# The next layer's modulation inside the first merge: condition rows in PSUM, loads two steps ahead, products to a buffer of their own, another count of steps per slot

## Chip, cores, metric

One core of one Trainium2 chip runs the whole program. The metric is the device time of one execution, in microseconds (us).

## What is computed

A backbone of two layers (DEPTH = 2) over 1024 latent tokens and 256 context tokens, width 1024, float32. Each layer normalises and modulates its input, projects it once, runs four token mixers r = 0..3 (pooling, latent attention, differential attention, windowed attention), gates and merges them and projects out:

```python
shift, scale, gate = jnp.split(jax.nn.silu(c) @ w_mod + b_mod, 3, axis=-1)
shift_c, scale_c, gate_c = jnp.split(jax.nn.silu(c_ctx) @ w_mod + b_mod, 3, axis=-1)
h = rms_norm(x, g_pre) * (1 + scale[:, None, :]) + shift[:, None, :]
z = split_cols(h @ w_in)
...
m = sum(mgate[:, :, r] * ((ys[r] * gates[:, :, r]) @ w_br[r]) for r in range(N_BRANCH))
x_new = x + gate[:, None, :] * rms_norm(m @ w_out, g_post)
```

mgate is the sigmoid of 4 x 1024 columns of z, gates the silu of 4 x 256 others. Two condition vectors, c and c_ctx, multiply the same w_mod: silu(c) and silu(c_ctx) are "the two condition rows". The gate of layer 0 (1024 columns) and shift, scale and gate of layer 1 (3072 columns) are needed only after the merge of layer 0, and it is these that the changed code computes.

## The kernel before

**The merge of layer 0** is one loop over 32 pairs (r, d), counted here as q = 0..31: branch r = q // 8, block d = q % 8 of 128 output columns. In each q TensorE makes three chunks of the gate projection (two of 512 columns, latent tokens, and one of 256, context), 24 matmuls of float32 each, into PSUM tiles pd (two buffers). ScalarE evicts each chunk through a sigmoid (function ev): sg for a chunk of 512 (three buffers), sgc for that of 256. Behind the first chunk of a q stand the branch products of the q before (branch_mm): small matmuls with bh and bl into the PSUM tiles pt and acc, which VectorE multiplies by the sigmoid (m<-sg,pt in r = 0, sg<-sg,pt later; sgc likewise) and, for r > 0, GpSimd adds to the sum (m<-m,sg). bh and bl are the rounded branch weights and their rest: ScalarE writes bh, VectorE bl. ScalarE and GpSimd also split the projection's weights (wh, then wl<-wraw,wh, 128x1024).

**The inputs ygs of the branch products** come from gated_y, a generator that is advanced between the chunks: loads of ya, yb, g, rb; then on VectorE ya<-ya,yb, ya<-ya,rb, ya<-ya,g, on ScalarE yt<-ya, on VectorE yt<-ya,yt. diff_norm does the norm of the third branch, with eight small matmuls (L1290) into columns 0 to 40 of p3s; to_rows transposes into another part of it. p3s is a PSUM tile of 128 x 1536 floats, free in this stage but for these two and the scratch below.

**The modulation** is the class RowMods. TensorE has no part in it: for each block of 128 output columns VectorE forms two dot products of a 128 x 512 tile of transposed weights (wmt) with the two condition rows, broadcast to all partitions (crow); `dot`, L149, is one tensor_tensor_reduce with a sum over the row. Rows of 1024 are taken in two halves hf of 512: in half 0 the sums go to mpart, in half 1 they start from mpart and end in msums, and put (L62 and L64) adds the bias into the layer's tables. With 32 blocks that are 64 steps, two products each. One step is

```python
hf, q = self.steps[self.at]
if q == 0:
    self.row(hf)
self.load(self.at)
self.load(self.at + 1)
w = self.w.pop(self.at)
for i in range(2):
    dot(self.jk, w, self.c[:, i], ...)
```

wmt has two buffers, so a load is issued one step ahead. row(hf), at the first step of each half, loads both rows into crow (one buffer in SBUF), lets ScalarE take the sigmoid into jk and VectorE multiply. jk is 512 columns of p3s in PSUM: the sigmoid's scratch and the place to which all products are written (they are not used; only their sums are). The merge loop calls rm.step() after each of the three chunks of q > 0, 93 times.

**What sets the order.** The program text gives the order in which instructions are handed to the framework's scheduler, which then places them on each engine by its own costs; calls under `late` keep their program order. Each engine runs its queue in order. DMAs are issued from SP's queue alone.

## Time and profile before

| what | before |
|---|---|
| median of 3 runs | 2775.82 us (2775.63 to 2791.7) |
| the profiled execution | 2784.56 us |
| its span in the trace | 2782.6 us |
| mean granted clock of TensorE | 0.972 |
| busy, share of the span | PE 94%, DVE 56%, ACT 43%, POOL 29% |

PE is TensorE's matmuls, PEld its weight loads, DVE VectorE, ACT ScalarE, POOL GpSimd, SP the engine that issues the DMAs. L150 is line 150 of the kernel. Names after the operation are out<-in; CUSTOM_DVE_ANT_0 at L150 is the product with its sum. In square brackets a row gives the time that the engine stood idle just before the instruction, and what ended it. PEclk is the clock that TensorE was granted, as a part of full speed. The span is from the first to the last instruction; the 2 us by which the execution is longer lie outside. The shares of busy time are means over the whole program; the modulation runs from about 820 to 1090 us of the span.

### The profile page before, as it was taken

To read this page: it belongs to the slowest core of one execution; us is meant where nothing else is said; L and a number is where in the kernel's file an instruction comes from. 1 tells how busy PE (TensorE), PEld (TensorE's weight loads), DVE (VectorE), ACT (ScalarE), POOL (GpSimd) and SP (SyncE) were. 2 spreads that over 40 slices of the span, in tenths; PEclk is the share of its full clock that TensorE was granted. 3 is DMA by queue.
4 is the path that set the end of the run, shared out by engine and by line. 5 is a ranking of instruction groups with operands and counts; after the bars stand their busy time and mean duration, and the time that the engine had idled before them with its cause. 6 is when DMAs were issued, how large, how long until landed. Compare 5 with 4: busy or idle time off the path is not lost.

```text
span 2782.6 us, 38390 instructions
## 1 busy us (share of the span) xinstructions
PE 2628.2 (94%) x14194; PEld 2216.5 (80%) x14194; DVE 1563.1 (56%) x2638; ACT 1184.7 (43%) x2176; POOL 816.8 (29%) x492
## 2 busy tenths in 40 slices
PE   7999998899999988999999998998999999999998
PEld 5777877788987877888878776777788988888878
DVE  7544888967555786333147653788866633233133
ACT  4433765665652211222145442776655732222231
POOL 4223434300012223334323322444100022444323
PEclk9999998999999999999999999999999999999999
DMA  6366324323443443221125367434323343222122
GB/s 234 111 194 195 117 84 138 115 84 94 120 129 120 156 138 121 76 76 61 37 84 173 112 189 216 135 92 136 110 77 104 90 133 110 78 82 89 48 76 99
DMA packets 209069, 322.27 MB, mean 116 GB/s; under 512 B 26740, under 2 KB 123634, under 8 KB 208882
## 3 DMA queue, kind: packets, MB, share of 16 engines
q1 hardware_dynamic: 208882, 319.83, 37.0%
q8 instruction: 111, 1.82, 0.3%
q14 instruction: 76, 0.62, 0.1%
HBM read 239.07 MB, written 77.86 MB: 114 GB/s over the span
## 4 chain that ended last, share of the span: by engine, by line
PE 71%; DVE 14%; DMA 5%; issue 4%; POOL 2%; ACT 2%; SPq 1%; POOLq 0%; DVEq 0%; ACTq 0%
PE pd L76 13%; PE pd L78 13%; PE pd L77 13%; PE acc L1013 6%; PE pt L997 5%; PE pt L76 2%; PE pss L1108 2%; PE pt L77 2%; PE pt L78 2%; DVE P L969 2%; DVE pss L150 2%; PE pss L1166 1%; DVE t L53 1%; PE pss L1067 1%; DMA wmt<-in_w_modt_dram 1%
## 5 line engine op out<-in xcount | busy, mean ns | idle before, releaser
L76 PE MATMUL pd<-h,wh 128*128 128x512 f32 (+2 forms) x2288 | 861.4, 377 | 36.3 <-ACT sg L50 23.2
L78 PE MATMUL pd<-h,wl 128*128 128x512 f32 (+2 forms) x2288 | 848.0, 371 | 0.3 <-POOL wl L53 0.3
L77 PE MATMUL pd<-h,wh 128*128 128x512 f32 (+2 forms) x2288 | 847.5, 370 | 0.5 <-DVE h L56 0.5
L53 POOL TENSOR_TENSOR wl<-wraw,wh 128x1024 fp32r<-128x1024 f32 x106 | 263.2, 2483 | 1010.0 <-ACT wh L50 787.4
L76 PEld LDWEIGHTS pd<-h,wh 128*128 128x128 f32 (+1 forms) x2288 | 438.4, 192 | 103.4 <-ACT sg L50 25.0
L78 PEld LDWEIGHTS pd<-h,wl 128*128 128x128 f32 (+1 forms) x2288 | 437.7, 191 | 69.6 <-issue 1.5
L77 PEld LDWEIGHTS pd<-h,wh 128*128 128x128 f32 (+1 forms) x2288 | 438.8, 192 | 60.7 <-DVE h L56 1.0
L969 DVE CUSTOM_DVE_ANT_0 P<-pss,zero 128x1280 f32<-128x1280 f32 (+1 forms) x216 | 295.5, 1368 | 120.3 <-PE pss L1108 61.8
L53 DVE TENSOR_TENSOR tl<-pt,th 128x512 fp32r<-128x512 f32 (+1 forms) x420 | 276.7, 670 | 113.3 <-ACT th L50 110.2
L50 ACT ACTIVATE th<-pt 128x512 fp32r<-128x512 f32 (+1 forms) x420 | 240.8, 582 | 183.9 <-PE pt L997 176.5
L53 DVE TENSOR_TENSOR sg<-sg,pt 128x512 f32<-128x512 f32 x96 | 65.2, 685 | 384.4 <-PE pt L78 384.4
L997 PE MATMUL pt<-kc,P 128*128 128x128 f32 x1632 | 256.2, 277 | 14.5 <-DVE P L56 9.0
L1013 PE MATMUL acc<-th,vt 128*128 128x256 f32 x816 | 246.0, 314 | 5.8 <-ACT th L50 5.1
L1013 PE MATMUL acc<-tl,vt 128*128 128x256 f32 x816 | 221.4, 292 | 7.2 <-DVE tl L53 7.1
L50 ACT ACTIVATE wh<-wraw 128x1024 fp32r<-128x1024 f32 x124 | 130.5, 1053 | 199.6 <-PE pd L77 149.8
L50 ACT ACTIVATE sg<-pd 128x512 f32<-128x512 f32 x128 | 75.6, 591 | 328.3 <-PE pd L78 301.2
L997 PEld LDWEIGHTS pt<-kc,P 128*128 128x128 f32 x1632 | 194.2, 143 | 25.5 <-DVE P L56 14.3
L50 ACT ACTIVATE P<-P,m 128x1280 f32<-128x1280 f32 (+1 forms) x144 | 182.7, 1269 | 70.6 <-DVE m L969 69.9
L53 POOL TENSOR_TENSOR m<-m,sg 128x512 f32<-128x512 f32 x96 | 132.9, 1390 | 207.2 <-DVE sg L53 206.0
L1013 PEld LDWEIGHTS acc<-th,vt 128*128 128x128 f32 x816 | 157.0, 192 | 36.7 <-ACT th L50 22.9
L1013 PEld LDWEIGHTS acc<-tl,vt 128*128 128x128 f32 x816 | 157.7, 193 | 21.2 <-DVE tl L53 14.0
L50 ACT ACTIVATE P<-P,negm 128x1280 f32<-128x1280 f32 (+3 forms) x144 | 146.6, 1018 | 31.2 <-DVE negm L969 30.2
(290 smaller groups left out, 3988.0 us busy)
## 6 DMA issues: line engine op xcount, KB each, us to landing
wraw<-in_w_in_dram SPq DMA_DIRECT2D x108, 512.0 KB, 3.6
wmt<-in_w_modt_dram SPq DMA_DIRECT2D x64, 256.0 KB, 2.9
wraw<-in_w_out_dram SPq DMA_DIRECT2D x32, 512.0 KB, 3.3
yd<-ot SPq DMA_DIRECT2D x108, 128.0 KB, 2.0
kt<-dkd SPq DMA_DIRECT2D x64, 160.0 KB, 3.3
qt<-dqd SPq DMA_DIRECT2D x72, 128.0 KB, 2.7
ya<-yd SPq DMA_DIRECT2D x36, 256.0 KB, 3.3
yb<-yd SPq DMA_DIRECT2D x36, 256.0 KB, 3.0
```

The costliest lines, as they stand in the source:

```text
L50: return nc.scalar.activation(out=o, in_=i, func=func, **kw)
L53: return (e or nc.vector).tensor_tensor(out=o, in0=a, in1=b, op=op)
L76: nc.tensor.matmul(ps, wh(k), xh(k), start=k == 0, stop=False)
L77: nc.tensor.matmul(ps, wh(k), xl(k), start=False, stop=False)
L78: nc.tensor.matmul(ps, wl(k), xh(k), start=False, stop=k == n - 1)
L150: nc.vector.tensor_tensor_reduce(out=jk, in0=a, in1=b, scale=1.0, scalar=start, op0=ALU.mult, op1=ALU.add, accum_out=o)
L969: nc.vector.tensor_tensor_reduce(out=o, in0=i, in1=zero.to_broadcast([128, nk]) if mask is None else mask, scale=-1.0, scalar=1e30 if h is ...
L997: t = nc.tensor.transpose(pt[:, 2 * j + i, :], Ps[i][:, (g + j) * 128:(g + j + 1) * 128], ident)
L1013: nc.tensor.matmul(acc, vt[:, kts[g + j], :], x[:, j, :], start=g + j == 0 and a == 0, stop=g + j == nk - 1 and a == 1)
L1067: nc.tensor.matmul(o, qt[0:96, 0, qs], kh[0:96, ks], start=True, stop=False)
L1108: last["s"] = nc.tensor.matmul(ps[:, b0 - k0:b0 - k0 + n], qt[:, mp, qs], kv[mp][:, b0:b0 + n], start=True, stop=True)
L1166: nc.tensor.matmul(ps[:, o0:o0 + n], qv[:, i, :], kv[a][:, k0:k0 + n], start=a == 0, stop=a == 1)
```

## The change

The list of steps is now 68 entries: before the 32 blocks of each half stand its two condition rows, as entries of their own (q < 0). A row comes through the same buffers and the same loads as a weight tile (wmt, now three buffers, loaded two entries ahead; the first two at the start). Its sigmoid goes to jk, now a tile in SBUF (mjunk), and its product to c, which is 1024 columns of PSUM (the last two thirds of p3s). The products of the dots go to mjunk in SBUF. step() runs as many entries as bring the count to slot x 68 // 66: with the 93 calls of the loop one entry per call, two at the 33rd and at the 66th, none behind. The transposed norm uses other columns of p3s.

```diff
@@ -182,47 +182,52 @@
     later = Later()
 
     class RowMods:
-        def __init__(self, js, p, jk):
-            self.js, self.p, self.jk = js, p, jk
+        def __init__(self, js, p, rows, slots):
+            self.js, self.p = js, p
+            self.jk = p.tile([128, 512], F, name="mjunk", bufs=1)
             self.part = p.tile([128, len(js), 2], F, name="mpart", bufs=1)
             self.sums = p.tile([128, len(js), 2], F, name="msums", bufs=1)
-            self.steps = [(hf, q) for hf in range(2) for q in range(len(js))]
-            self.c = None
-            self.at = 0
+            self.c = rows.rearrange("p (c n) -> p c n", c=2)
+            self.order = []
+            for hf in range(2):
+                self.order += [(hf, i - 2) for i in range(2)] + [(hf, q) for q in range(len(js))]
+            self.slots = slots
+            self.slot = self.at = 0
             self.w = {}
+            for n in range(2):
+                self.load(n)
 
         def load(self, n):
-            if n < len(self.steps) and n not in self.w:
-                hf, q = self.steps[n]
-                l, j = self.js[q]
-                w = self.p.tile([128, 512], F, name="wmt", tag="wmt", bufs=2)
-                dma(w, A["w_modt"][l, j, :, hf * 512:hf * 512 + 512])
-                self.w[n] = w
-
-        def row(self, hf):
-            self.c = self.p.tile([128, 2, 512], F, name="crow", tag="crow", bufs=1)
-            for i in range(2):
-                c, e = self.c[:, i], self.jk
-                dma(c, A["cr"][i:i + 1, hf * 512:hf * 512 + 512].broadcast_to([128, 512]))
-                act(e, c, AF.Sigmoid)
-                tt(c, c, e, ALU.mult)
+            if n < len(self.order):
+                hf, q = self.order[n]
+                cols = slice(hf * 512, hf * 512 + 512)
+                w = self.w[n] = self.p.tile([128, 512], F, name="wmt", tag="wmt", bufs=3)
+                if q < 0:
+                    dma(w, A["cr"][q + 2:q + 3, cols].broadcast_to([128, 512]))
+                else:
+                    l, j = self.js[q]
+                    dma(w, A["w_modt"][l, j, :, cols])
 
         def step(self):
-            if self.at >= len(self.steps):
+            self.slot += 1
+            while self.at < min(len(self.order), self.slot * len(self.order) // self.slots):
+                self.run()
+
+        def run(self):
+            hf, q = self.order[self.at]
+            self.load(self.at + 2)
+            w = self.w.pop(self.at)
+            self.at += 1
+            if q < 0:
+                act(self.jk, w, AF.Sigmoid)
+                tt(self.c[:, q + 2], w, self.jk, ALU.mult)
                 return
-            hf, q = self.steps[self.at]
-            if q == 0:
-                self.row(hf)
-            self.load(self.at)
-            self.load(self.at + 1)
-            w = self.w.pop(self.at)
             for i in range(2):
                 dot(self.jk, w, self.c[:, i], self.part[:, q, i:i + 1] if hf else 0.0,
                     (self.sums if hf else self.part)[:, q, i:i + 1])
             if hf:
                 l, j = self.js[q]
                 mods[l].put(j, self.sums[:, q])
-            self.at += 1
 
     def col_rs(acc, n, p):
         nt = n // 128
@@ -1297,7 +1302,7 @@
             msf = ms.rearrange("p h t -> p (h t)")
             tt(msf, msf, nhalf[:, 0:4 * nq], ALU.pow, nc.gpsimd)
             yield 9.0
-            to_rows(msf, 4 * nq, rdd[2, 0:4 * nq], p3s[:, 512:1024])
+            to_rows(msf, 4 * nq, rdd[2, 0:4 * nq], p3s[:, 256:512])
 
         def gated_y(r, j):
             for c0, n in qch:
@@ -1363,7 +1368,7 @@
         prep.tick(0.0)
         st.load((l, W_M))
 
-        rm = RowMods([(0, 16 + q) for q in range(KT)] + [(1, q) for q in range(3 * KT)], rp, p3s[:, 1024:1536]) if l == 0 else None
+        rm = RowMods([(0, 16 + q) for q in range(KT)] + [(1, q) for q in range(3 * KT)], rp, p3s[:, 512:1536], 66) if l == 0 else None
 
         def some(body, n):
             for _ in range(n):
```

On ScalarE, around the condition rows of the second half, before: sgy is the sigmoid of gated_y, yt its output, pss<-crow the rows' two sigmoids.

```order
L50 ACTIVATE sg<-pd 128x512
L50 ACTIVATE bh<-braw 128x256
L50 ACTIVATE sgy<-g 128x512
L50 ACTIVATE sg<-pd 128x512
L50 ACTIVATE wh<-wraw 128x1024
L50 ACTIVATE sgc<-pd 128x256
L50 ACTIVATE pss<-crow 128x512 x2
L50 ACTIVATE sg<-pd 128x512
L50 ACTIVATE sgy<-g 128x512
L50 ACTIVATE yt<-ya 128x512
```

And there after the change, where mjunk<-wmt are the rows' sigmoids.

```order
L50 ACTIVATE sg<-pd 128x512
L50 ACTIVATE bh<-braw 128x256
L50 ACTIVATE sgy<-g 128x512
L50 ACTIVATE mjunk<-wmt 128x512 x2
L50 ACTIVATE sg<-pd 128x512
L50 ACTIVATE wh<-wraw 128x1024
L50 ACTIVATE sgc<-pd 128x256
L50 ACTIVATE sg<-pd 128x512
L50 ACTIVATE sgy<-g 128x512
L50 ACTIVATE yt<-ya 128x512
```

The two sigmoids stood behind sgc of the q and now stand ahead of its sg; the evictions sg and sgc are behind them.

On VectorE, at the end of the first half, before: sums to mpart are half 0, sums to msums half 1, crow<-crow,pss x2 the rows' products (two instructions, one row of the list).

```order
L53 TENSOR_TENSOR ya<-ya,rb 128x512
L150 ISA pss,mpart<-wmt,crow 128x512
L150 ISA mpart 128x1
L53 TENSOR_TENSOR ya<-ya,g 128x512
L150 ISA pss,mpart<-wmt,crow 128x512
L150 ISA mpart 128x1
L150 ISA pss,mpart<-wmt,crow 128x512
L150 ISA mpart 128x1
L150 ISA pss,mpart<-wmt,crow 128x512
L150 ISA mpart 128x1
L53 TENSOR_TENSOR crow<-crow,pss 128x512 x2
L150 ISA pss,msums<-wmt,crow,mpart 128x512
```

And there after the change, where the products read their condition row from pss (PSUM) and write mjunk (SBUF), and pss<-wmt,mjunk x2 are the rows' products.

```order
L150 ISA mjunk,mpart<-wmt,pss 128x512
L150 ISA mpart 128x1
L53 TENSOR_TENSOR ya<-ya,rb 128x512
L150 ISA mjunk,mpart<-wmt,pss 128x512
L150 ISA mpart 128x1
L53 TENSOR_TENSOR ya<-ya,g 128x512
L53 TENSOR_TENSOR pss<-wmt,mjunk 128x512 x2
L150 ISA mjunk,msums<-wmt,pss,mpart 128x512
L150 ISA msums 128x1
L150 ISA mjunk,msums<-wmt,pss,mpart 128x512
L150 ISA msums 128x1
```

Of the four row products that stood between ya<-ya,rb and the rows, one is left, ahead of ya<-ya,g; the rows come right behind that. Row products in all stay 128, puts stay 32. The orders on TensorE and GpSimd do not change. On SP the loads of a row now stand two entries ahead of its use, among those of the weights, and 68 loads go through the tile wmt.

## Rows read from the trace of the kernel before

**Rows 1.** busy time by stretches, us (count) per engine; PEclk: granted clock.

```profile
950.00:1000.00 50.00, 39.11 (x186) 32.60 (x185) 40.69 (x82) 9.28 (x17) 10.16 (x6) 0.90 0.46 147
```

**Rows 2.** timeline of ScalarE, bh rows: start, duration (us), instruction, idle before, releaser.

```profile
860.60 0.42 ACT L50 ACTIVATE bh<-braw 128x256 fp32r<-128x256 f32 x1 [4.33 <-PE acc L77]
...
921.56 0.42 ACT L50 ACTIVATE bh<-braw 128x256 fp32r<-128x256 f32 x1 [2.22 <-PE acc L77]
...
956.06 0.42 ACT L50 ACTIVATE bh<-braw 128x256 fp32r<-128x256 f32 x1 [2.74 <-PE acc L77]
...
1005.10 0.42 ACT L50 ACTIVATE bh<-braw 128x256 fp32r<-128x256 f32 x1 [2.78 <-PE acc L77]
...
1040.77 0.42 ACT L50 ACTIVATE bh<-braw 128x256 fp32r<-128x256 f32 x1 [2.83 <-PE acc L77]
...
1088.05 0.42 ACT L50 ACTIVATE bh<-braw 128x256 fp32r<-128x256 f32 x1 [0.68 <-PE acc L77]
```

**Rows 3.** timeline of TensorE, 850 to 1060 us: its waits.

```profile
854.24 1.05 PE L1290 MATMUL pss<-kc,yb 128*128 128x2 f32 x8 [1.59 <-ACT yb L50]
...
965.03 0.50 PE L76 MATMUL pd<-h,wh 128*128 128x512 f32 x1 [0.57 <-ACT sg L50]
...
993.13 0.80 PE L76 MATMUL pd<-h,wh 128*128 128x512 f32 x1 [9.41 <-ACT sg L50]
...
1058.51 0.79 PE L76 MATMUL pd<-h,wh 128*128 128x512 f32 x1 [9.36 <-ACT sg L50]
```

**Rows 4.** timeline of ScalarE, 970 to 1060 us: its waits.

```profile
977.55 0.60 ACT L50 ACTIVATE pss<-crow 128x512 f32<-128x512 f32 x1 [11.25 <-DMA crow<-in_cr_dram]
...
991.97 0.63 ACT L50 ACTIVATE yt<-ya 128x512 fp32r<-128x512 f32 x1 [10.07 <-DVE ya L53]
...
1057.34 0.63 ACT L50 ACTIVATE yt<-ya 128x512 fp32r<-128x512 f32 x1 [15.63 <-DVE ya L53]
```

**Rows 5.** timeline of VectorE and GpSimd, 960 to 1062 us.

```profile
963.58 0.68 DVE L53 TENSOR_TENSOR m<-sg,pt 128x512 f32<-128x512 f32 x1
...
1018.47 0.23 DVE L62 TENSOR_SCALAR ab<-msums,kc 128x2 f32<-128x2 f32 x1
...
1018.61 0.75 DVE L150 CUSTOM_DVE_ANT_0 pss<-wmt,crow,mpart 128x512 f32<-128x512 f32 x1
...
1019.46 0.76 DVE L150 CUSTOM_DVE_ANT_0 pss<-wmt,crow,mpart 128x512 f32<-128x512 f32 x1
...
1049.26 0.68 DVE L53 TENSOR_TENSOR sg<-sg,pt 128x512 f32<-128x512 f32 x1
...
1059.53 2.37 POOL L53 TENSOR_TENSOR wl<-wraw,wh 128x1024 fp32r<-128x1024 f32 x1 [4.04 <-issue]
...
1059.54 2.39 DVE L64 TENSOR_SCALAR ab<-msums,kc 128x2 f32<-128x2 f32 x1
```

**Rows 6.** tile wmt: row products (ns: min/median/max) and its loads.

```profile
L150 DVE CUSTOM_DVE_ANT_0 pss<-wmt,crow x64: 686/700/2947, 827.5 to 973.6; 128x512 f32<-128x512 f32 x64
...
L150 DVE CUSTOM_DVE_ANT_0 pss<-wmt,crow,mpart x64: 746/758/2708, 980.8 to 1087.4; 128x512 f32<-128x512 f32 x64
...
DMA to landing us min/median/max: 2.4/2.9/5.3
```

**Rows 7.** VectorE groups by shape, 820 to 1090 us: busy us, mean ns, idle.

```profile
L150 DVE CUSTOM_DVE_ANT_0 pss<-wmt,crow 128x512 f32<-128x512 f32 x64 | 57.4, 897 | 26.3 <-DMA wmt<-in_w_modt_dram 14.4 <-PE pss L1290 10.6
...
L150 DVE CUSTOM_DVE_ANT_0 pss<-wmt,crow,mpart 128x512 f32<-128x512 f32 x64 | 55.0, 860 | 9.3 <-DMA wmt<-in_w_modt_dram 8.4
...
L53 DVE TENSOR_TENSOR ya<-ya,g 128x512 f32<-128x512 f32 x7 | 4.8, 686 | 0.1
```

**Rows 8.** tile sg, 820 to 1090 us, columns as in rows 6.

```profile
L53 DVE TENSOR_TENSOR sg<-sg,pt x10: 677/680/686, 1003.5 to 1089.0; 128x512 f32<-128x512 f32 x10
...
L53 POOL TENSOR_TENSOR m<-m,sg x9: 1264/1301/1743, 1004.2 to 1089.2; 128x512 f32<-128x512 f32 x9
```

**Rows 9.** tile crow: its DMA's time to landing.

```profile
DMA to landing us min/median/max: 5.6/5.6/5.6
```

## The prediction

> **What bounds the kernel now.** I read the table by stretches first, for the stretch in which the modulation runs. Between 950 and 1000 us TensorE is busy 39.1 of 50 us at a granted clock of 0.90, and VectorE is busy 40.7 [rows 1]. The rest of the program is not touched by the change, so everything has to come out of this stage. Next the rows in which ScalarE splits the branch weights (bh): each waits for TensorE's last product of one q, so their starts are a clock of the stage. From 921.56 to 956.06 two q's take 34.50 us, 17.25 each, with TensorE never idle [rows 2]. Against that pace three stretches are too long [rows 2]:
> - 860.60 to 921.56, three q's: 60.96 - 51.75 = 9.2 us;
> - 956.06 to 1005.10, two q's: 49.04 - 34.50 = 14.5 us;
> - 1005.10 to 1088.05, four q's: 82.95 - 69.00 = 13.95 us.
>
> TensorE's own timeline says where: it waits 1.59 us for ScalarE before eight small products of the norm (L1290), with a second wait of this kind in the first stretch, and 9.41 and 9.36 us for ScalarE's eviction sg [rows 3]. ScalarE's timeline says why: before 991.97 it waited 10.07 us, and before 1057.34 it waited 15.63 us, for VectorE's product ya, with sg queued behind it [rows 4]. So TensorE waits for a VectorE that is late. How late, VectorE's timeline shows: its first product of q=6 starts at 963.58 and that of q=10 at 1049.26 [rows 5], while TensorE had finished all products of these q's at 956.06 and 1040.77 [rows 2]; lateness 7.5 and 8.5 us, counted from the bh row.
>
> TensorE can take 8.3 us of such lateness: after 956.06 it ran two more chunks and first stood still at 964.46, 0.57 us before 965.03 [rows 2, 3]. The first product and the eviction behind it take 0.7 + 0.6 us, so a plain q stalls from a lateness of 7.0 us; 7.5 gave the 0.57. Where a chain of y products stands before the eviction in ScalarE's queue, the first product to TensorE's restart took 1058.51 - 1049.26 = 9.25 us [rows 3, 5], and a lateness of 8.5 cost 8.5 + 9.25 - 8.3 = 9.4 us, as measured.
>
> VectorE is late for three reasons. The 128 row products (L150) wait 14.4 and 8.4 us for the weights' DMA [rows 7]; they have a median of 0.700 and 0.758 us but means of 0.897 and 0.860 [rows 6, 7], so 64 x 0.197 + 64 x 0.102 = 19.1 us are stretches, the longest row 2.9 us. What stretches them is seen best in a two-column put, all in SBUF: 2.39 us at 1059.54 beside a GpSimd instruction of 2.37 us from 1059.53, where the one at 1018.47 took 0.23 [rows 5]. And at the half's end ScalarE waits 11.25 us, until 977.55, for the first of the condition rows [rows 4], and VectorE for ScalarE.
>
> **The change part by part.**
> Rows in PSUM, products to SBUF. VectorE's products that read one operand from PSUM stay between 677 and 686 ns, though GpSimd's sums of the first fall beside the second, from 1004.2 on [rows 8]; so a row product with its row in PSUM should not be stretched. I cost it at the medians and take all of the 19.1 us off VectorE. Not seen is this very operation with a PSUM operand; nearest are sg<-sg,pt at a median of 0.680 and ya<-ya,g, all in SBUF, at 0.686 [rows 7, 8], so 0 us per product, between 0 and the old stretch of 0.1 to 0.2 on the mean. What stays exposed are the puts behind each second product (L62, L64), as the one at 1059.54 [rows 5].
> The Trainium skill, VectorE: DVE Perf Modes, in its section "The TRN2 errata — SBUF-src ops pay a fixed extra latency per instruction", gives a PSUM source 120 cycles of fixed cost against 58 for SBUF, 0.065 us at 0.96 GHz. The two rows just named show no such difference; by the rule 17 products of a q would take 1.1 us longer and the last term below would be 0, the time 2760.
>
> Loads two ahead. A load still waits for the products of three steps back, and takes 2.9 us to land [rows 6]; with the issue I count 3.4 us until its product can start. Before, one step (two products, 1.6 to 1.9 us) covered it, so a run of steps went at 2.6 to 2.8 us; now two cover it. I take the 22.8 us of DMA waits off but for about 0.2 us a step in the first half. GpSimd has no DMA of this; on SP, y loads stand behind one more weight load. The one that matters, ya of q=7, is again issued when VectorE has finished the step just before it, as before.
>
> Rows as steps of their own. The first pair gains nothing: it comes at the same place. The second pair's DMA is now two steps ahead, but it may only start when the buffers three steps back are free, lands 5.6 us later [rows 9], and ScalarE now has both sigmoids before sg instead of behind sgc (order above). From VectorE's first product of q=6 I count: second row issued after 2.3 us of VectorE work, landed 6.0 us later (0.4 to issue), sigmoid 0.6 and sg 0.6: TensorE can go on 9.5 us after that product.
>
> Even steps. The order does not spread them. Counted between one sgc product and the next, q=3 to q=9 held 10, 14, 15, 9, 11, 15, 14 row products and now hold 12, 15, 19, 13, 13, 17, 17; q=10 and 11 held 12 and 8, now 6 and 0. So VectorE's work per q rises to TensorE's pace: q=8 has 17 products at 0.85 (1018.61 to 1019.46 [rows 5]), 9 puts at 0.14 to 0.2 (1018.47 to 1018.61) and four other operations of 1.9 together: 17.9 us, and about 1.5 for puts and splits that meet GpSimd: 19.4 against 17.25.
>
> **The sum**, in the three stretches:
> 1. Norm products. The gaps before them follow on stretched row products and DMA waits; with these gone VectorE is through before TensorE arrives. After the gap at 854.24 the clock is low for a while, and that goes too. The small products stay (1.05 us for eight [rows 3]). Of 9.2 I take 5; bounds 2 and 6.
> 2. The half's end. Lateness at q=6: q=4 starts about on time, q=4 and q=5 take 17.5 to 18 us each, so 0.5 instead of 7.5. Stall there 0.5 + 9.5 - 8.3 = 1.7. q=6 holds the rows and 13 products, some 20.4 us, so lateness at q=7 is 0.5 + 20.4 - 17.25 - 1.7 = 2.0; its y chain needs 7.2 us, stall 0.9. With a microsecond of low clock 3.6 of 14.5 remain. Gain 11; bounds 5 and 14.
> 3. The y chain of q=10. Lateness at q=8 about 3, and two q's of 19.4 add 2.2 each: 7.4 at q=10, hardly less than the 8.5 of before. Stall 7.4 + 8.6 - 8.3 = 7.7, and about 3 for the low clock behind it, as 13.95 - 9.36 = 4.6 was lost beside the long wait before: 10.7 of 13.95 remain. Gain 3; bounds -3 and 13.9.
>
> Together 5 + 11 + 3 = 19 us: the profiled execution's 2784.6 would become 2765.6. It lies 8.8 us above the median of the runs shown, 2775.8, so I forecast 2757. A measurement of this kernel tells about 1% (28 us) from no change; 19 us is less.
>
> **The rivals.**
> A. VectorE catches up. If puts and splits meet GpSimd rarely and loads are never late, q=8 and q=9 take about 17.3 us, lateness at q=10 is 2 to 3 and the stall goes. For it: the products' stretches were two thirds of all stretch here. Against: the puts. Gain 6 + 14 + 11 = 31, time 2745.
> B. Slower. ScalarE's sigmoids ahead of sg turn each microsecond of lateness at q=6 into a stall of TensorE, as there is no slack left. If the products are stretched as before, or slower with their new operands, lateness at q=6 is some 9: stall 10.2, low clock 3, 2 at q=7 makes 15.2 of 14.5; the longer runs of products make lateness at q=10 some 13, 13.3 + 3 = 16.3 of 13.95; the norm products gain 1. Net 2 slower, 2778. It decides from a lateness of 8 at q=6. Against it stand the unstretched PSUM rows [rows 8].
> C. The change does not spread the steps, and bunching gives most back: rows arrive late (stall 4 at q=6, 3 at q=7 with the clock 8 remain), the y chain of q=10 is unchanged or 2 worse, norm products gain 4: gain 4 + 6.5 - 1 = 10, time 2766.
>
> **How the numbers follow.** Forecast 0.60, A 0.20, C 0.15, B 0.05. The forecast's terms between their bounds give gains of 4 to 34; A and C lie inside 2745 to 2766. I leave out the outer ends: 2744 to 2771. Faster by over 1% (under 2748.1) is A alone: 0.20. Slower by over 1% would be over 2803.6, which no case reaches: 0.03 for what I don't see. Within 1%: 0.77.
>
> **What would show it.** Right: row products of the second half at 0.76 us with no row over 1 us, DMA waits of L150 under 6 us, the norm's gaps gone; between the bh rows of q=6 and q=8 some 38 us; and one long wait of TensorE for sg left, of 5 to 9 us, behind a late first product of q=10, with the clock low behind it. A would show as no wait over 3 us there; B as products stretched again and a wait of over 8 us at q=6. The forecast is wrong if VectorE's first product of q=10 starts less than 4 us after the end of TensorE's products, or if the wait at the second rows is above 4 us.

## The result

| | before | after |
|---|---|---|
| median of 4 runs each | 2777.57 us (2775.63 to 2791.7) | 2755.22 us (2746.41 to 2758.63) |
| ratio, 95% interval | | 0.9898 (0.9875 to 0.9922) |
| the profiled execution, its span | 2784.56, 2782.6 us | 2752.67, 2750.5 us |
| mean granted clock of TensorE | 0.972 | 0.977 |
| PE, DVE, ACT, POOL busy | 94, 56, 43, 29% | 95, 56, 43, 29% |

By the medians the kernel became 22.4 us faster, 0.8%: 2755 where 2757 was forecast. The ratio says 1.0%, with an interval of 0.8 to 1.25%.

The same views of the profile after show where it came from. First the clock of the stage, the rows of ScalarE in which bh is written as soon as TensorE has finished the products of one q; they answer to [rows 2].

```profile
855.02 0.42 ACT L50 ACTIVATE bh<-braw 128x256 fp32r<-128x256 f32 x1 [2.76 <-PE acc L77]
...
909.64 0.42 ACT L50 ACTIVATE bh<-braw 128x256 fp32r<-128x256 f32 x1 [2.22 <-PE acc L77]
...
944.15 0.42 ACT L50 ACTIVATE bh<-braw 128x256 fp32r<-128x256 f32 x1 [2.74 <-PE acc L77]
...
961.40 0.42 ACT L50 ACTIVATE bh<-braw 128x256 fp32r<-128x256 f32 x1 [1.70 <-PE acc L77]
...
981.62 0.42 ACT L50 ACTIVATE bh<-braw 128x256 fp32r<-128x256 f32 x1 [1.20 <-PE acc L77]
...
998.99 0.42 ACT L50 ACTIVATE bh<-braw 128x256 fp32r<-128x256 f32 x1 [2.83 <-PE acc L77]
...
1016.31 0.42 ACT L50 ACTIVATE bh<-braw 128x256 fp32r<-128x256 f32 x1 [2.83 <-PE acc L77]
...
1059.95 0.42 ACT L50 ACTIVATE bh<-braw 128x256 fp32r<-128x256 f32 x1 [2.78 <-DMA wraw<-in_w_in_dram]
```

Against 17.25 us per q the three stretches are now too long by 54.62 - 51.75 = 2.9, 37.47 - 34.50 = 3.0 and 78.33 - 69.00 = 9.3 us, where they were by 9.2, 14.5 and 13.95: 6.3, 11.5 and 4.6 us less, 22.5 in all. The two profiled executions lie 31.9 us apart, so that the 22.5 found here and the 22.4 between the medians agree by accident. Of the other 9.4 us, 3.2 lie between the bh rows of q = 0 and q = 1, where the gap of 1.59 us at 854.24 [rows 3] stood and the same small products now wait 0.16 us (below; L1295 by this kernel's lines). That this is the change isn't shown: the same stretch takes 18.4 us before and 15.2 after, but 16.3 in a second execution of the changed kernel (e5 below) and 15.5 in a kernel with the old operands (e7). The rest, 2.4, 0.3 and 3.7 us, lies ahead of the bh row of q = 0, between q = 12 and the last q, and behind the merge.

TensorE's waits, answering to [rows 3]:

```profile
850.23 1.05 PE L1295 MATMUL pss<-kc,yb 128*128 128x2 f32 x8 [0.16 <-ACT yb L50]
...
972.46 0.50 PE L76 MATMUL pd<-h,wh 128*128 128x512 f32 x1 [2.66 <-ACT sg L50]
...
1031.38 0.80 PE L76 MATMUL pd<-h,wh 128*128 128x512 f32 x1 [6.69 <-ACT sg L50]
```

The two long ones are 2.66 and 6.69 us, where they were 9.41 and 9.36. VectorE's first products of q = 6, 7, 8, 9 and 10, answering to the first and fifth of [rows 5]:

```profile
944.53 0.68 DVE L53 TENSOR_TENSOR m<-sg,pt 128x512 f32<-128x512 f32 x1
...
965.30 1.28 DVE L53 TENSOR_TENSOR m<-sg,pt 128x512 f32<-128x512 f32 x2
...
983.71 0.68 DVE L53 TENSOR_TENSOR sg<-sg,pt 128x512 f32<-128x512 f32 x1
...
1003.63 0.68 DVE L53 TENSOR_TENSOR sg<-sg,pt 128x512 f32<-128x512 f32 x1
...
1022.40 0.68 DVE L53 TENSOR_TENSOR sg<-sg,pt 128x512 f32<-128x512 f32 x1
```

Against the bh rows from 944.15 to 1016.31 VectorE is late by 0.4, 3.9, 2.1, 4.6 and 6.1 us. Before it was late by 7.5 at q = 6 and 8.5 at q = 10. q = 8 took it 1003.63 - 983.71 = 19.9 us. ScalarE's rows at the half's end and before the two restarts answer to [rows 4]:

```profile
949.54 0.63 ACT L50 ACTIVATE mjunk<-wmt 128x512 f32<-128x512 f32 x1 [4.46 <-DVE mpart L150]
...
950.94 0.63 ACT L50 ACTIVATE mjunk<-wmt 128x512 f32<-128x512 f32 x1 [0.77 <-DVE pss L53]
...
951.48 0.58 ACT L50 ACTIVATE sg<-pd 128x512 f32<-128x512 f32 x1
...
971.30 0.63 ACT L50 ACTIVATE yt<-ya 128x512 fp32r<-128x512 f32 x1 [9.47 <-DVE ya L53]
...
1030.21 0.63 ACT L50 ACTIVATE yt<-ya 128x512 fp32r<-128x512 f32 x1 [12.96 <-DVE ya L53]
```

The rows' two sigmoids now run at 949.54 and 950.94, and sg follows at once; the wait of 11.25 us for a row is gone. What is left are the waits for ya, 9.47 and 12.96 us. Last the row products in the view of the tile wmt, as minimum, median and maximum in ns, answering to [rows 6].

```profile
L150 DVE CUSTOM_DVE_ANT_0 mjunk<-wmt,pss x64: 669/686/691, 845.9 to 948.8; 128x512 f32<-128x512 f32 x64
L150 DVE CUSTOM_DVE_ANT_0 mjunk<-wmt,pss,mpart x64: 732/743/749, 954.1 to 1035.5; 128x512 f32<-128x512 f32 x64
```

And VectorE's groups by shape between 820 and 1090 us (busy us, mean ns, idle before), answering to [rows 7]; the third row is the readout of the sum behind each product.

```profile
L150 DVE CUSTOM_DVE_ANT_0 mjunk<-wmt,pss,mpart 128x512 f32<-128x512 f32 x64 | 47.6, 743 | 3.1 <-DMA wmt<-in_w_modt_dram 2.1
L150 DVE CUSTOM_DVE_ANT_0 mjunk<-wmt,pss 128x512 f32<-128x512 f32 x64 | 43.9, 685 | 14.3 <-PE pss L1295 8.8 <-DMA wmt<-in_w_modt_dram 3.9
...
L150 DVE DVE_READ_ACCUMULATOR2_ANT mpart<- 128x1 f32 x64 | 5.3, 82 | 0.0
```

None of the 128 takes over 0.75 us, where the longest took 2.9. The waits for weights in these groups fell from 14.4 + 8.4 to 3.9 + 2.1 us. The table by stretches, answering to [rows 1], shows the same from afar: full clock and TensorE busy 47.3 of 50 us where it was 39.1, and what is lost now in the next row.

```profile
950.00:1000.00 50.00, 47.34 (x249) 40.55 (x248) 45.53 (x108) 11.70 (x22) 12.67 (x8) 1.00 0.56 178
1000.00:1050.00 50.00, 43.31 (x217) 36.78 (x216) 41.81 (x93) 8.12 (x15) 18.26 (x13) 0.93 0.43 135
```

### The profile page after: what moved, and what is told of

Read it like the earlier page. It is cut to its first block, busy times and chain, and to the rows that moved or that the text cites. A ratio compares the mean times of both kernels' runs of the same rounds, so it can differ in the third digit from the quotient of the medians.

```text
span 2750.5 us, 38390 instructions
## 1 busy us (share of the span) xinstructions
PE 2615.1 (95%) x14194; PEld 2208.5 (80%) x14194; DVE 1539.2 (56%) x2638; ACT 1185.3 (43%) x2176; POOL 810.2 (29%) x492
## 4 chain that ended last, share of the span: by engine, by line
PE 72%; DVE 14%; DMA 4%; issue 4%; ACT 3%; POOL 2%; SPq 1%; POOLq 0%; DVEq 0%; ACTq 0%
PE pd L76 14%; PE pd L78 14%; PE pd L77 14%; PE acc L1018 6%; PE pt L1002 5%; PE pss L1113 2%; PE pt L76 2%; PE pt L77 2%; PE pt L78 2%; DVE P L974 2%; DVE mjunk L150 2%; PE pss L1171 1%; PE pss L1072 1%; DVE t L53 1%; PE pss L1074 1%
## 5 line engine op out<-in xcount | busy, mean ns | idle before, releaser
L1002 PE MATMUL pt<-kc,P 128*128 128x128 f32 x1632 | 255.8, 277 | 14.4 <-DVE P L56 8.8
L1002 PEld LDWEIGHTS pt<-kc,P 128*128 128x128 f32 x1632 | 193.7, 142 | 25.1 <-DVE P L56 13.8
L1018 PEld LDWEIGHTS acc<-tl,vt 128*128 128x128 f32 x816 | 156.9, 192 | 19.7 <-DVE tl L53 12.8
```

The costliest lines, as they stand in the source:

```text
L1002: t = nc.tensor.transpose(pt[:, 2 * j + i, :], Ps[i][:, (g + j) * 128:(g + j + 1) * 128], ident)
L1018: nc.tensor.matmul(acc, vt[:, kts[g + j], :], x[:, j, :], start=g + j == 0 and a == 0, stop=g + j == nk - 1 and a == 1)
```

## The experiments

Each kernel is given with the three stretches of its profiled execution: A (norm), B (half's end) and C (y chain of q = 10) are what the time between the bh rows of q = 1, 4, 6, 8 and 12 has over 17.25 us per q, read as above. "ahead" is the number of row products, of 128, that start before VectorE's first product of q = 10, "weights" all its waits for weights. Ratios are to the kernel before on the same chip, whose medians were 2784.3 us for e1 to e4, 2781.2 for e5 to e8 and 2780.5 for e9 to e11; kernels of different groups are compared by their ratios.

| kernel | median us | ratio (95%) | A | B | C | ahead | weights us |
|---|---|---|---|---|---|---|---|
| before | 2777.6 | 1 | 9.2 | 14.5 | 13.95 | 108 | 22.9 |
| after | 2755.2 | 0.9898 (0.9875 to 0.9922) | 2.9 | 3.0 | 9.3 | 121 | 6.0 |
| e5, after again | 2756.6 | 0.9909 (0.9895 to 0.9922) | 2.9 | 5.2 | 5.2 | 121 | 6.7 |
| e1, one ahead | 2754.3 | 0.9903 (0.9886 to 0.9920) | 2.9 | 7.2 | 4.9 | 101 | 32.2 |
| e2, old operands, one ahead | 2776.7 | 0.9970 (0.9956 to 0.9983) | 9.1 | 13.3 | 14.2 | 104 | 28.4 |
| e3, mixed operands | 2765.6 | 0.9931 (0.9915 to 0.9946) | 2.9 | 10.0 | 10.6 | 127 | 10.4 |
| e4, rows late | 2755.7 | 0.9896 (0.9881 to 0.9910) | 2.9 | 6.8 | 6.7 | 117 | 6.2 |
| e6, spread | 2745.4 | 0.9868 (0.9853 to 0.9883) | 3.2 | 0.0 | 0.6 | 56 | 0 |
| e7, spread, old operands | 2759.2 | 0.9922 (0.9909 to 0.9935) | 9.8 | 0.0 | 8.1 | 56 | 12.4 |
| e8, puts from PSUM | 2757.2 | 0.9911 (0.9897 to 0.9924) | 2.9 | 4.9 | 3.8 | 116 | 8.1 |
| e9, spread, no p3s | 2756.5 | 0.9909 (0.9894 to 0.9924) | 2.9 | 0.0 | 7.4 | 56 | 103.5 |
| e10, e7 from q = 5 | 2745.0 | 0.9866 (0.9849 to 0.9882) | 2.9 | 0.0 | 1.1 | 40 | 19.7 |
| e11, e6 from q = 5 | 2745.2 | 0.9866 (0.9846 to 0.9886) | 2.9 | 0.0 | 0.3 | 40 | 0.4 |

(In e3 one bh row is late behind ScalarE's own work; its B is taken from TensorE's last product instead.)

### e1: loads one entry ahead

```diff
-                w = self.w[n] = self.p.tile([128, 512], F, name="wmt", tag="wmt", bufs=3)
+                w = self.w[n] = self.p.tile([128, 512], F, name="wmt", tag="wmt", bufs=2)
...
-            self.load(self.at + 2)
+            self.load(self.at + 1)
```

> The changed kernel with the loads one entry ahead and two weight buffers, as before the change; rows in PSUM and products in SBUF stay. Theory 'VectorE's time' (every microsecond taken off VectorE between 820 and 1090 us counts alike, whatever it was): the change took 21 us of stretches, about 8 us of shorter spacing behind a product and 17 us of waits for weights off VectorE; this run gives the 17 back and keeps 29 of 46, so about 2764 us, VectorE's waits for weights at 15 to 25 us, TensorE's wait for sg near q = 10 at 8 to 11 us instead of 6.7. Rival 'loads': the waits for weights were the whole point, and the time goes back to 2774 or more. Rival 'operands': the stretches were, the waits fall into idle time, and the time stays within 3 us of 2755.

From the tile wmt: its second-half products, and the idle time of VectorE (us, times) that ended with the weights' landing.

```profile
L150 DVE CUSTOM_DVE_ANT_0 mjunk<-wmt,pss,mpart x64: 732/746/750, 972.6 to 1074.7; 128x512 f32<-128x512 f32 x64
...
  DMA wmt<-in_w_modt_dram: 32.2, 26
```

VectorE waited 32.2 us for weights, more than before the change, and the time did not move by what the intervals (some 5 us either way) can tell: 0.9903 beside 0.9909 for e5. So of the three "operands" holds for the time ("VectorE's time" missed by 10 us), and the shorter waits by themselves were worth nothing that shows. But they do not fall into idle time either. With the loads one ahead the scheduler places fewer steps early: 101 row products ahead of q = 10 instead of 121. 20 products at 0.785 are 15.7 us of VectorE that then run behind the y chain; the waits ahead of it are 26.4 us where e5 has 6.7, so 19.7 more. That the two nearly cancel is arithmetic; no run keeps one without the other. Two loads ahead bought VectorE time, and the order spent most of it on more products before the same chain.

### e2: and the old operands

```diff
-            self.jk = p.tile([128, 512], F, name="mjunk", bufs=1)
+            self.jk = rows[:, 0:512]
...
-            self.c = rows.rearrange("p (c n) -> p c n", c=2)
+            self.c = p.tile([128, 2, 512], F, name="crow", bufs=1)
```

> As the run before it, and with the condition rows back in SBUF and the products back in PSUM; of the change only the rows as steps of their own and the step count stay. Theory 'VectorE's time': nothing of the 46 us is kept, while the bunched order stays, so 2773 to 2782 us, row products stretched to 2 us and more again, 11 us or more slower than the run with one entry ahead alone. Rival 'operands': nearly all of the 22 us are lost in this run, and next to none in the other. Rival 'loads': this run is within 4 us of the other.

The tile wmt of e2:

```profile
L150 DVE CUSTOM_DVE_ANT_0 pss<-wmt,crow,mpart x64: 745/760/2967, 984.5 to 1090.8; 128x512 f32<-128x512 f32 x64
```

These are its second-half products in the tile wmt: stretched to 2.97 us again. The kernel is 22.4 us slower than e1, so three quarters of the 30 us between the kernel before and e1 on this chip hang on the operands, as long as the steps stand where they do (e10 has them elsewhere). By itself this run fits "VectorE's time" as well as "operands"; e1 decides between them. What is left of the change, rows as steps, stands at 0.9970, 7.6 us by the medians; in the trace A, B and C are together only 1.1 us below those of before, so most of it lies elsewhere and stays unexplained.

### e3: which operand does it

```diff
-            self.jk = p.tile([128, 512], F, name="mjunk", bufs=1)
+            self.jk = rows[:, 512:1024]
...
-            self.c = rows.rearrange("p (c n) -> p c n", c=2)
+            crow = p.tile([128, 512], F, name="crow", bufs=1)
+            self.c = [rows[:, 0:512], crow]
...
-                dot(self.jk, w, self.c[:, i], ...
+                dot(w if i else self.jk, w, self.c[i], ...
```

> The changed kernel with its two products of a step put into different memories: the first reads its row from PSUM and writes PSUM, the second reads its row from SBUF and writes SBUF (over the weights, which nothing reads afterwards). With the kernel before (SBUF row, PSUM products) and the changed one (PSUM row, SBUF products) this fills a table of four. If the row's place decides on the stretch by GpSimd, the first product never takes over 0.75 us and the second reaches 2 us or more; if the place of the products decides, the first is stretched and the second not. If the place of the products decides on the spacing behind a product, the first stands 0.06 us further from its successor than the second, with a readout of 0.14 us against 0.08; if the row's place does, it is the other way round. Time: half of the stretches come back, about 10 us of VectorE, so some 2758 to 2763 us.

The four kinds of product, from the tile wmt of e3 (ns: min/median/max):

```profile
L150 DVE CUSTOM_DVE_ANT_0 pss<-wmt,pss x32: 684/690/697, 848.0 to 953.4; 128x512 f32<-128x512 f32 x32
L150 DVE CUSTOM_DVE_ANT_0 wmt<-wmt,crow x32: 680/691/2120, 848.8 to 954.7; 128x512 f32<-128x512 f32 x32
L150 DVE CUSTOM_DVE_ANT_0 pss<-wmt,pss,mpart x32: 741/750/757, 960.9 to 1033.5; 128x512 f32<-128x512 f32 x32
L150 DVE CUSTOM_DVE_ANT_0 wmt<-wmt,crow,mpart x32: 734/746/2822, 961.7 to 1034.8; 128x512 f32<-128x512 f32 x32
```

The row's place decides on the stretch: with the row in PSUM the maximum is 0.697 and 0.757 us though the products go to PSUM, with the row in SBUF it is 2.1 and 2.8 though they go to SBUF. The place of the products decides on the readout behind them: 0.14 us where they write PSUM (the kernel before, and the first products here), 0.08 where they write SBUF (the changed kernel, and the second products here). The spacing differs more than was expected: from a first product to the second 0.783 us (median, first half), from a second to the next first 0.618. At 2765.6 us the time came a little above the range, about halfway between e1 and e2.

The Trainium skill, SBUF — State Buffer, in its section "Who interferes with whom", has the rule that a VectorE instruction with two SBUF inputs contends with a GpSimd instruction that reads SBUF; these four rows agree with it. The rule weighed in the prediction, the Trainium skill's VectorE: DVE Perf Modes, section "The TRN2 errata — SBUF-src ops pay a fixed extra latency per instruction", does not show: a product from a PSUM row takes 690 ns, from an SBUF row 691, and with products to SBUF both times 686 (changed kernel) and 691.

### e4: rows loaded at their step

```diff
+            if q < 0:
+                self.load(self.at, True)
```

(load() otherwise leaves out entries with q < 0.)

> The changed kernel with the four loads of condition rows issued only when their step comes, not two entries ahead. Theory: the second pair is then on the path, VectorE and ScalarE wait some 5 us for it near 950 us with sg queued behind its sigmoids, and TensorE stands 3 to 6 us there, so 2759 to 2763 us and a second long wait for sg. Rival: VectorE has caught up before it, the wait falls into idle time, and the time stays within 3 us of 2755.

TensorE's two long waits, from its timeline in e4:

```profile
975.71 0.80 PE L76 MATMUL pd<-h,wh 128*128 128x512 f32 x1 [4.91 <-ACT sg L50]
...
1034.11 0.79 PE L76 MATMUL pd<-h,wh 128*128 128x512 f32 x1 [4.60 <-ACT sg L50]
```

The wait at the half's end came as expected, 4.91 us; the time did not, 0.9896, and stayed within 3 us of 2755 as the rival has it, though the wait did not fall into idle time. C fell from 9.3 to 6.7 us, and the second wait is 4.60 instead of 6.69. Here is a thing that the theory lacked: while TensorE stands, VectorE catches up. Its lateness was 5.8 us at q = 7 and 0.3 at q = 8 (profiled run of the change: 3.9 and 2.1), and 4.1 at q = 10 instead of 6.1. So a microsecond lost at q = 7 is in part paid back at q = 10.

How much of such a difference is chance can be seen in e5, the changed kernel once more, with B and C of 5.2 and 5.2 instead of 3.0 and 9.3. Its two waits, from TensorE's timeline:

```profile
978.91 0.52 PE L76 MATMUL pd<-h,wh 128*128 128x512 f32 x1 [2.61 <-ACT sg L50]
...
1035.73 0.50 PE L76 MATMUL pd<-h,wh 128*128 128x512 f32 x1 [3.00 <-ACT sg L50]
```

And its bh row (ScalarE) and VectorE's first product of q = 10:

```profile
1024.35 0.42 ACT L50 ACTIVATE bh<-braw 128x256 fp32r<-128x256 f32 x1 [2.83 <-PE acc L77]
...
1026.67 0.68 DVE L53 TENSOR_TENSOR sg<-sg,pt 128x512 f32<-128x512 f32 x1
```

VectorE is 2.3 us late at q = 10, where it was 6.1. About half of the 3.8 between them it had made up by q = 8, where it was 0.15 late instead of 2.1 after a B longer by 2.2 us. Most of the rest is q = 8 itself, 18.4 us instead of 19.9: in the profiled run one put there met a GpSimd instruction and took 1.95 us, in e5 the longest took 0.91.

### e5 to e7: spreading the steps

e5 is the changed kernel. e6 pins each step's first product behind what was handed to VectorE before it (`dot` now returns its instruction for that); e7 does the same to e2.

> The changed kernel once more, beside the three runs that follow. All theories: as in the result, 0.990 of the kernel before.

```diff
-                dot(self.jk, w, self.c[:, i], ...
+                d = dot(self.jk, w, self.c[:, i], ...
+                if i == 0:
+                    late(d)
```

> The changed kernel with the first product of each step pinned behind everything that the program has handed to VectorE before it. By the order 6 row products then stand between one sgc product and the next from q = 2 to q = 22 (10 and none around the second rows, 8 at the last), instead of 12 to 19 from q = 4 to q = 10. Theory 'bunching': what the changed kernel still loses between q = 5 and q = 13 (2.97 and 9.33 us over TensorE's pace) is VectorE's lateness from too many steps ahead of the y chains, so nearly all of it goes: 9 to 13 us below the changed kernel, no wait of TensorE for sg over 2 us, first products never more than 2 us behind TensorE. Rival 'y chain': the wait at q = 10 belongs to the chain of y products itself (9.25 us from a first product to TensorE's restart before the change), and 5 us or more of it stay; the gain is below 6 us. Rival 'pins': VectorE now stands at pinned products for weights or rows, and the time is that of the changed kernel or more.

The first product of q = 10, from VectorE's timeline in e6:

```profile
1020.45 0.69 DVE L53 TENSOR_TENSOR sg<-sg,pt 128x512 f32<-128x512 f32 x1 [9.98 <-PE pt L78]
```

VectorE stood 9.98 us idle and waited for TensorE, where in the changed kernel it was 6.1 us late. B and C are gone, with 0.58 us left; 11.2 us below e5 by the medians. "Bunching" holds, and of the two rivals nothing shows: no wait of TensorE for sg in this stage reaches 0.5 us. The chain of y products costs TensorE nothing when VectorE is on time.

> The kernel with condition rows in SBUF, products in PSUM and loads one entry ahead, with the same pins: spread steps and nothing else of the change. Theory 'bunching': stretched products cost only where VectorE is late, and with 6 products per q it is not (6 x 0.85 and some 11 us of other work in 17.25 us), so this run stands within 5 us of the run with pins alone and below the changed kernel by 4 us or more; only the gaps before the norm's small products, 9.2 us before the change, may keep some 2 to 4 us. Rival 'operands': the stretched products go on costing, and the time stays above the changed kernel's.

This one missed by 9 us: 2759.2 is 13.8 above e6, and level with the changed kernel or a little above it (0.9922 beside 0.9909; the intervals overlap). B is gone with stretched products as well, as expected. But A is 9.8, and C is 8.1, most of it at the second rows, which stand at q = 11 here and with one buffer less come late. In e7 ScalarE waited for the second of them, with sg behind it, and TensorE at the y chain that follows; from the timelines of the two:

```profile
1041.95 0.60 ACT L50 ACTIVATE pss<-wmt 128x512 f32<-128x512 f32 x1 [3.63 <-DMA wmt<-in_cr_dram]
...
1055.61 0.80 PE L76 MATMUL pd<-h,wh 128*128 128x512 f32 x1 [5.16 <-ACT sg L50]
```

### e8: the puts

```diff
-            self.sums = p.tile([128, len(js), 2], F, name="msums", bufs=1)
+            self.sums = sums.rearrange("p (n c) -> p n c", c=2)
```

(sums are 64 columns of p3s.)

> The changed kernel with the sums of the second half (msums) in PSUM, so that the two-column puts read one operand from PSUM. Theory: an operand in PSUM keeps an instruction from being stretched by GpSimd, also a small one, so no put takes over 0.6 us and 6.9 us of stretch go off VectorE, most of it before q = 10: TensorE's waits for sg shrink by 3 to 6 us in all. Rival: GpSimd then meets the next SBUF instruction instead (bl, ya), and the time stays within 2 us.

Puts of the changed kernel between 820 and 1090 us, from the view of the tile kc (min/median/max ns):

```profile
L64 DVE TENSOR_SCALAR gt<-msums,kc x16: 283/289/1552, 955.7 to 1036.3; 128x2 f32<-128x2 f32 x16
L62 DVE TENSOR_SCALAR ab<-msums,kc x8: 217/228/1946, 978.9 to 996.7; 128x2 f32<-128x2 f32 x8
```

The same groups in e8:

```profile
L64 DVE TENSOR_SCALAR gt<-pss,kc x16: 268/280/281, 961.4 to 1042.3; 128x2 f32<-128x2 f32 x16
L62 DVE TENSOR_SCALAR ab<-pss,kc x8: 203/219/220, 985.2 to 1002.3; 128x2 f32<-128x2 f32 x8
```

No put is stretched any more, the longest is 281 ns instead of 1946. The time is that of e5, as the rival has it, and the 3 to 6 us off TensorE's waits did not come: the two are 2.2 and 2.8 us, 2.6 and 3.0 in e5. As B and C are 8.7 us together beside 10.4 in e5, a microsecond or two may be won; the intervals are too wide to tell.

### e9 to e11: what A is

A stayed 9 us in e2 and e7 and was 3 in every kernel so far with its rows, or half of them, in PSUM. VectorE's timeline in the kernel before, at the second and third of the norm's groups:

```profile
866.52 0.70 DVE L150 CUSTOM_DVE_ANT_0 pss<-wmt,crow 128x512 f32<-128x512 f32 x1 [4.64 <-PE pss L1290]
...
871.14 2.38 DVE L150 CUSTOM_DVE_ANT_0 pss<-wmt,crow 128x512 f32<-128x512 f32 x1 [0.94 <-DMA wmt<-in_w_modt_dram]
...
874.23 0.14 DVE L150 DVE_READ_ACCUMULATOR2_ANT mpart<- 128x1 f32 x1
```

TensorE's timeline there, and at the last group:

```profile
865.98 0.50 PE L1290 MATMUL pss<-kc,yb 128*128 128x2 f32 x4
...
874.52 1.02 PE L1290 MATMUL pss<-kc,yb 128*128 128x2 f32 x8 [0.95 <-DVE mpart L150]
...
895.81 0.58 PE L1290 MATMUL pss<-kc,yb 128*128 128x2 f32 x4 [1.72 <-DVE mpart L150]
```

At 866.52 a row product starts 0.04 us after four small products of the norm end (865.98 + 0.50). At 874.52 eight small products start 0.15 us after the readout of the row product before them ends (874.23 + 0.14): TensorE stood 0.95 us for row products, one of them stretched to 2.38 us. At 895.81 it stood 1.72 us for another. The granted clock was 0.83 from 870 to 880 and from 890 to 900 us, where after the change it is 1.00; by these numbers 0.95 + 1.72 idle and some 2 x 10 x 0.17 = 3.4 at the low clock, 6.1 of the 6.3 us by which A differs. Neither side reads what the other writes. Both touch the PSUM tile p3s, in different columns. e2 and e7, with stretched products in p3s as well, have the same two gaps (0.94 and 1.64, 0.95 and 2.33 us).

```diff
-            self.c = rows.rearrange("p (c n) -> p c n", c=2)
+            self.c = p.tile([128, 2, 512], F, name="crow", bufs=1)
...
-                w = self.w[n] = self.p.tile([128, 512], F, name="wmt", tag="wmt", bufs=3)
+                w = self.w[n] = self.p.tile([128, 512], F, name="wmt", tag="wmt", bufs=1)
```

(with the pins of e6; the products stay in mjunk; each load is issued behind the products of the step before)

> The kernel with spread steps, its condition rows and its products both in SBUF and one weight buffer, so that no row product touches the PSUM tile p3s, in which the norm's small products (L1290 before the change) have their 40 columns. In the traces these small products start right behind a row product's readout, and row products right behind them. Theory 'shared tile': with old operands the gaps before the small products (9.8 us over the pace between q = 2 and q = 5 in the run with spread steps and old operands) come from this mutual waiting with stretched row products; here the row products are as stretched as there (up to 2 us and more), yet the gaps go: 2.5 to 4 us over the pace between q = 2 and q = 5. Rival 'stretch': a late VectorE makes the gaps by itself, and 7 us or more stay. One buffer makes the second pair of rows late: 5 to 12 us over the pace between q = 9 and q = 13 in either case, so the time is 2750 to 2760 us under the first, 2757 to 2767 under the second.

From the tile wmt of e9, the products of the first half:

```profile
L150 DVE CUSTOM_DVE_ANT_0 mjunk<-wmt,crow x64: 673/692/2862, 837.4 to 1040.0; 128x512 f32<-128x512 f32 x64
```

Stretched to 2.86 us, and A is 2.9. With one buffer VectorE waited 103.5 us for weights, and few of the stretched products fall beside the norm; but one does, and shows the point by itself. From VectorE's and TensorE's timelines in e9:

```profile
872.41 2.43 DVE L150 CUSTOM_DVE_ANT_0 mjunk<-wmt,crow 128x512 f32<-128x512 f32 x1 [0.88 <-DMA wmt<-in_w_modt_dram]
...
874.74 0.95 PE L1297 MATMUL pss<-kc,yb 128*128 128x2 f32 x8
```

The eight small products (L1297 in this kernel) start at 874.74 without a wait, while the stretched row product still runs (872.41 + 2.43 = 874.84). So TensorE's wait comes from the shared tile. (No run puts the row products into another PSUM tile. That it is the tile and not PSUM at large is argued: what releases TensorE is the readout of a product with which it shares only p3s.) It needs both: in the changed kernel, e3 and e6 row products still read or write p3s, but those that do aren't stretched, and A is 2.9 to 3.2. The tie itself is still there, on the other side: VectorE waited 8.8 us for the small products after the change (<-PE pss L1295 in the groups above), 10.6 before [rows 7], at no cost to TensorE. C of e9, 7.4, is in the range expected for the late rows, and so is the time.

e10 is e7, and e11 is e6, with the first step at q = 5:

```diff
-                if rm and q > 0:
+                if rm and q > 4:
```

(and 54 slots instead of 66)

> The kernel with spread steps and old operands (rows in SBUF, products in PSUM), with the steps starting only at q = 5, when the norm's small products are through, and 8 products per q instead of 6. Theory 'shared tile': without row products beside them the small products have no gaps, 2.5 to 4 us over the pace between q = 2 and q = 5, and the time is some 6 us below the same kernel with the early start, 2751 to 2755 us, if the second rows still cost their 8. Rival: the gaps have another cause and the time stays at 2757 or more.

> The changed kernel with pinned steps, starting only at q = 5. Theory: nothing is left to win, since with rows in PSUM the small products have no gaps worth naming (3.2 us over the pace in the run with pins and the early start, 2.9 in the changed kernel, and these are the small products themselves): within 3 us of the run with the early start, 0.987 of the kernel before. Rival: row products still hold the small products up, and 2 us or more come off.

e10 fell below its range, to 2745.0: A went as expected, and the 8 us of the second rows went too, which was not expected. These now stand at q = 13, behind C, where no y chain follows; from ScalarE's timeline in e10, one of the two and the bh row of q = 13:

```profile
1060.69 0.60 ACT L50 ACTIVATE pss<-wmt 128x512 f32<-128x512 f32 x1 [1.85 <-DMA wmt<-in_cr_dram]
...
1066.54 0.42 ACT L50 ACTIVATE bh<-braw 128x256 fp32r<-128x256 f32 x1 [2.68 <-issue]
```

The bh row of q = 12 is at 1049.17, so that q = 13 took 17.37 us with a late row in it: 0.1 over the pace. Of the 1.1 that are left in C, 0.9 lie between the bh rows of q = 10 and q = 11. e11 came as expected, 0.9866 beside 0.9868 for e6. With its row products stretched and its loads one ahead e10 is as fast as e11, 0.9866 for both (some 5 us either way), and A, B and C are 4.1 us together beside 3.2. So the old operands cost about a microsecond in these stretches, once the steps stand where nothing waits for them.

## Why the prediction was right, and where it was not

The sum was 5 + 11 + 3 = 19; measured 6.3 + 11.5 + 4.6 = 22.5. The first term lies a little above its bounds (2 to 6), the others within theirs. What was said of the order held in the profiled run: bunched before q = 10, one long wait left (6.69, forecast 5 to 9), the low clock behind it (9.3 - 6.69 = 2.6, forecast 3).

How the last two terms share the gain is luck. In e5, the same kernel, they are 14.5 - 5.2 = 9.3 and 13.95 - 5.2 = 8.8; the wait at q = 10 is 3.00 us, and VectorE's first product there 2.3 us late, less than the 4 us that the prediction names as a sign of being wrong. What holds in both executions is their sum, 16.1 and 18.1 where 14 was forecast, and the rule for a stall, lateness and chain less 8.3: at q = 10 it gives 6.1 + 8.6 - 8.3 = 6.4 in the profiled run (measured 6.69), 2.6 in e5 (3.00) and 4.4 in e4 (4.60). The lateness itself hangs on which puts meet GpSimd.

Of the rivals, A ("catches up") did not happen by itself, though e5 is halfway there; e6 made it happen, and 2745 was its time. B needed stretched products, and there were none. C expected too little: its rows would have left 8 at the half's end (3.0 and 5.2 measured), and the y chain got better, not worse. Whether the gain is "within 1%" (0.77) or just over it (0.20, given to A alone) the ratio's interval does not tell.

By its own steps:

- **Rows in PSUM.** Right on the stretches: median 0.686 and 0.743, maxima 0.691 and 0.749. Not seen: the products' new place shortens the readout from 139 ns (row below) to 82 (groups above). With it a product follows the one before after 0.730 and 0.784 us instead of 0.793 and 0.849 (medians over pairs that touch): 0.064 x 128 = 8.2 us of VectorE. "17 products at 0.85" was too much by 1.1 us for q = 8, and stretches of other instructions took that back by luck: 19.9 us measured, 19.4 forecast, 18.4 in e5.
- **Loads two ahead.** The waits fell as forecast (22.8 to 6.0 us). The prediction counted the shorter waits and the fuller q's as two things; e1 shows that they come together: with the waits back, 20 fewer products stand before the same chain, and the time is the same.
- **The second rows.** "TensorE can go on 9.5 us after that product" was 951.48 + 0.58 - 944.53 = 7.5. No wait at q = 6 (forecast 1.7), and so no rest for VectorE there: lateness at q = 7 3.9 (forecast 2.0) and the wait there 2.66 (forecast 0.9). Together 2.66 beside 2.6: right in sum by luck, as a wait that did not come at q = 6 left more of one at q = 7.
- **The norm's products.** The gain came, the reason was half of it. The prediction took the gaps of the first stretch for the kind at 854.24, a wait for ScalarE; the two in it, 0.95 and 1.72 us, are waits for VectorE's readout, and the wait at 854.24 stands ahead of the stretch. That VectorE is late there was not enough: e9 has a stretched product there and no gap. TensorE waits for stretched row products because both sides touch p3s.
- **Even steps.** That the order does not spread them was read rightly from it; e6 shows what spreading is worth: 11 us.
- **The rule on PSUM sources** (the Trainium skill, as weighed in the prediction) would have made the third term 0 and the time 2760; the products took no longer, and the term was 4.6 (8.8 in e5).

The readout before, in VectorE's groups by shape between 820 and 1090 us:

```profile
L150 DVE DVE_READ_ACCUMULATOR2_ANT mpart<- 128x1 f32 x64 | 8.9, 139 | 0.0
```

## What to carry to other kernels

Work that nobody waits for is not free where it stands in an in-order queue: look which chain stands behind it, and place it where none does, before making it cheaper. Here moving the products behind the chains (2745, ratio 0.987) was worth more than making them unstretched (2755, 0.990), and did not need it. Small pieces of one PSUM tile lent to two engines' unrelated work can tie the two together: look for waits between instructions that share no data. And take a second execution before reading single waits: those at q = 10 were 6.69 and 3.00 us in two executions of one kernel whose times differ by 4.5.

## Not expected of the hardware

The readout behind a summed product took 138 to 140 ns on the mean where the products went to PSUM (whether the row lay in PSUM or SBUF) and 80 to 82 ns where they went to SBUF, again for both; with the products in SBUF and the sums in PSUM (second half of e8) it took 142. A put of two columns took up to 2.39 us beside GpSimd with its tensor in SBUF [rows 5] and at most 0.28 us with it in PSUM (e8).
